# Opening's row sums, split bias loads and earlier row products in a one-core decoder block

## The chip, the core and the metric

The kernel runs on one core of one Trainium2 chip. The time of a run is the device time of one execution in microseconds (us). PE is the matrix engine (its weight loads are listed apart, as PEld), DVE the vector engine, ACT the scalar engine, POOL the GpSimd engine, and SP the queue that issues the transfers (DMA) of the weights.

## The reference

One decoder block for 256 tokens of width 1024, in f32. Cut to what matters:

```python
h = rmsnorm(x, g) * (1 + scale(c)) + shift(c)     # scale, shift, gates: silu(c) @ W_ada, row products
z = h @ W_in                                      # q, k's, v's, NSA gates, MLA latents, merge gates
kc = gelu(blocks(k) @ w1) @ w2                    # compression; vc alike
o  = NSA(q, kc, vc, k_slc, ..) + T5 bias in each logit
m  = MLA(latents)                                 # 8 heads
x1 = x + gate * (merge(o, m) @ W_o)
y  = x1 + gate2 * ffn(norm(x1) modulated)         # gate branch with causal conv of width 3, silu
```

`W_ada` is [1024, 6 * 1024]. A row product multiplies one 128 x 1024 piece of it by silu(c) on DVE and sums along the row: one column of `mod` each.

## The kernel before, in words

Each f32 matrix product is made of three products of a high and a low part (`hi` on ACT, `lo` on DVE). The tokens lie along the free axis, 256 of them; the width is tiled by 128, so that k runs from 0 to 7.

The stages, with their times in the profile: opening (to 16 us): `opening()` squares x on ACT, adds pairs of tiles on DVE (L316), sums the rows with 1-column matmuls on PE (`ssq.reduce`, tile `ms`), `rstd_col` makes the inverse root (ACT, then a power on POOL, L272), `rstd_bc` writes it on a diagonal (ACT, L279) and broadcasts it with one matmul (`ms<-sq,ones`). `busy(n)` issues n matmuls whose result nobody reads (`lg<-ones`); their numbers stand in `WARM`. `modulate(k)` makes the row products of tile k (`gemv`, L375), its scale column `am` (ACT, L402), its shift (L407) and the modulated tile `hf`, and from it the parts `hh[k]`, `hl[k]`.

Then the products with k = 0 to 7 (16 to 62 us), weights `wA` streaming; values and gates (63 to 80 us): eight pieces `wvg` of 280 KB, 12 matmuls for each k, with the query tiles evacuated between them (L441, L442). Up to here the order of each engine is that of the code. `fetch()` issues the next piece on SP; its buffer is one of a ring of five, so an issue waits until DVE has made the low part of the piece that lay there. The T5 bias is read back from `vdr` in DRAM in four transfers of 512 KB (L521) into the tiles `BT`; attention reads them at L905.

From 80 us a scheduler orders the instructions by priorities. Attention of the first token mixer runs in pairs by `ORDER`; between its steps stands other work in the order of `WORK`: C0 to C3 (products of the compression, weights `cw` and `wc`, tile `ms` for C0), L, N, M (latents), and A, one row product (`ada_rest`) of the 32 pieces `adaR`. `ada_load` issues a piece into a ring of two (`ADB`), after `mark`. Then come the MLA heads (L1027 and around), the row products still left, the output projection, the feed-forward part (243 to 452 us) and the tail.

SP issues all transfers in one order. The program also makes an issue wait for the transfer eight issues before it.

Of the kernel before, what the change touches and what calls it, by code (L numbers as in the profile page):

```python
# [9 lines left out]
F32 = mybir.dt.float32  # L10
F32R = mybir.dt.float32r
I32 = mybir.dt.int32
AF = mybir.ActivationFunctionType
# [20 lines left out]
C_MASK, C_VM, C_ROWV, C_IF, C_SGN = 0, 384, 392, 393, 394  # L34
N_CST = 395

WARM = (5, 2, 2, 3, 3)
PD = 4
ENG2 = "vv"
LATE = 1  # L40
# [7 lines left out]
PK = "W D G LG TT EX SC TU PC V PJ EQ ET EK EV TB CM ME TA".split()  # L48
TAE = "pp"
TE = "aaaavvaa"  # L50
WORK = "C0 A A A A A A A L0 C1 L1 A C2 A L2 C3 N M0 KR CK CS M1 A CR M2 Q0 CL UK A A Q1 M3 M7 M5 M6 UV M4"
ORDER = "T00 L00 L01 T01 F L10 V00 F V01 F L11 T11 T10 F V10 F V11 C"


def body(tc, a, out, dbg=None):
    nc = tc.nc
    with ExitStack() as ctx:
# [20 lines left out]
        def s4(dt, shape=(128, 4, 256)):  # L78
            return sp.tile(list(shape), dt, tag="s4", name=nm("s4"))
# [112 lines left out]
        def mm(o, l, r, start, stop, **kw):  # L192
            nc.tensor.matmul(o, l, r, start=start, stop=stop, **kw)  # L193
# [74 lines left out]
        def rstd_col(ssq, width):  # L268

            v = tp.tile([128, 4], F32, tag="rv", name=nm("rv"))  # L270
            nc.scalar.activation(v[:, 0:2], ssq.ps[:, 0:2], AF.Identity, scale=1.0 / width, bias=eps[:])
            nc.gpsimd.tensor_tensor(v[:, 2:4], v[:, 0:2], mhalf[:], ALU.pow)  # L272
            return v[:, 2:4]
# [12 lines left out]
        def busy(n):  # L286

            for i in range(n):
                mm(warm[:, 0:128], ones[:], ones[:], True, True)

        cond = cp.tile([128, 8], F32, name="cond")
        crow = cp.tile([128, 1024], F32, name="crow")
        ssq = Squares(4)
        xsq = big(F32)
        psv = bank("o")
        vdr = dp.tile([16, 384], F32, name="vdr")
# [2 lines left out]
        def opening():  # L299

            nc.scalar.activation(cth[:], par[:, C_C:C_C + 8], AF.Tanh, scale=0.5)
            nc.vector.scalar_tensor_tensor(cond[:], cth[:], 1.0, par[:, C_C:C_C + 8], ALU.add, ALU.mult)
            nc.vector.tensor_scalar(cond[:], cond[:], 0.5, None, ALU.mult)

            busy(WARM[0])
            for c in range(2):
                ps = bank("pt")
                for i in range(4):
                    mm(ps[:, i * 128:i * 128 + 128], free(cond[:, 4 * c + i:4 * c + i + 1], [[0, 128]]), ident, True, True)
                nc.vector.tensor_copy(crow[:, c * 512:c * 512 + 512], ps[:])  # L310
            for h in range(2):
                busy(WARM[1 + h])
                for j in range(2):
                    t = xsq.t[h][:, 2 * j:2 * j + 2, :]
                    nc.scalar.activation(t, xT.t[h][:, 2 * j:2 * j + 2, :], AF.Square)
                    nc.vector.tensor_tensor(t[:, 0, :], t[:, 0, :], t[:, 1, :], ALU.add)  # L316
                    ssq.reduce(t[:, 0, :], h == 0 and j == 0, h == 1 and j == 1)
            mm(psv[0:16, 0:384], tabx[:], oneh[:], True, True)

        rst = t1("rst", bufs=1)  # L320

# [72 lines left out]

        def modulate(k, r=None):

            for j in (1, 0):
                gemv(mod[:, 8 * j + k:8 * j + k + 1], ads.pop((k, j))[:])
            am = tp.tile([128, 1], F32, tag="am", name=nm("am"))
            if r is None:  # L400
                v = rstd_col(ssq, D)
            nc.scalar.activation(am[:], mod[:, 8 + k:9 + k], AF.Identity, scale=par[:, C_GMIX + k:C_GMIX + k + 1],  # L402
                                 bias=sb1[:, k:k + 1])
            if r is None:
                r = rstd_bc(ssq, D, v=v)
                busy(WARM[4])
            nc.scalar.activation(mod[:, k:k + 1], mod[:, k:k + 1], AF.Identity, bias=par[:, C_ADAB + k:C_ADAB + k + 1])  # L407
            hfs[k] = t1("hf")
            nc.vector.scalar_tensor_tensor(hfs[k][:], xT[:, k, :], am[:], r, ALU.mult, ALU.mult)
            return r  # L410
# [61 lines left out]

        with tc.manual_schedule(engines={EN.DVE, EN.Activation, EN.PE, EN.SP}):
            opening()
            rsp = modulate(0)
            head()
            one = dict(skip_group_check=True)

            def products(k, c, w):
                wh, wl = w  # L480
                tiles = [(8 * c + m, slice(m * 128, m * 128 + 128)) for m in range(8)]
                if k == 0:

                    for x, y in ((wh, hh), (wh, hl), (wl, hh)):
                        for mt, sl in tiles:
                            mm(accp(mt), x[:, sl], y[:, k, :], x is wh and y is hh and mt % 2 == 0, False, **one)
                else:
                    for mt, sl in tiles:
                        mm3(accp(mt), wh[:, sl], wl[:, sl], hh[:, k, :], hl[:, k, :], False, k == 7, **one)

            for k in range(8):
                part_hi(k)
                if k == 0:
                    nc.scalar.activation(rst[:], rsp, AF.Copy)
                    nc.scalar.activation(vec[:], psv[0:16, 0:384], AF.Copy, scale=-1.0)
                    nc.gpsimd.dma_start(vdr[:], vec[:])
                if k < 5:
                    fetch_ada(k + 3)
                    fetch()
                    fetch()  # L500
                if k == 0:
                    part_lo(k)
                w = rest()
                if k:
                    part_lo(k)
                head()
                products(k, 0, w)
                if k < 6:
                    w = rest()
                    head()  # L510
                    products(k, 1, w)
                if k < 7:
                    modulate(k + 1, rst[:])

            fetch()
            fetch()
            fetch()
            BT = [[s4(F32) for _ in range(2)] for _ in range(2)]
            vd = vdr[:]
            for i in range(4):  # L520
                nc.sync.dma_start(BT[i // 2][i % 2][:], bass.AP(tensor=vd.tensor, offset=vd.offset + i * 4 * 384,  # L521
                                                                  ap=[[1, 128], [384, 4], [1, 256]]))
            w = rest()
            head()
            products(6, 1, w)
            w = rest()
            products(7, 1, w)
            for gp in range(2):
                for br in (1, 0):
                    k_evac(br, gp)  # L530
            for i in range(2):
                head()
                pending.append(rest())
            t_evac(0)
            t_evac(1)


            VST = s4(F32, (128, 2, 2, 4, 64))
            gate = cp.tile([128, 2, 48], F32, name="gate")
            vps = [bank(t) for t in ("lg", "lg", "pt", "pt")]  # L540
            queries = [(i, j) for i in (1, 3, 2, 0) for j in range(2)]
            for k in range(8):
                wh, wl = pending.pop(0)
                if k < 5:
                    mark = fetch()

                for tt in (1, 0):
                    for c in range(2):
                        sl = slice(c * 280, (c + 1) * 280)
                        o = vps[tt * 2 + c][:, 0:280]  # L550
                        ts_ = slice(tt * 128, tt * 128 + 128)
                        mm(o, hh[:, k, ts_], wh[:, sl], k == 0, False)
                        mm(o, hl[:, k, ts_], wh[:, sl], False, False)
                        mm(o, hh[:, k, ts_], wl[:, sl], False, k == 7)
                if k < 6:
                    head()
                    pending.append(rest())
                i, j = queries.pop(0)
                q_evac(i, (j,))
            for tt in (1, 0):  # L560
                for c in range(2):
                    ps = vps[tt * 2 + c]
                    nc.scalar.activation(VST[:, tt, c, :, :], ps[:, 0:256].rearrange("p (g d) -> p g d", g=4), AF.Copy)
                    ga = nc.scalar.activation(gate[:, tt, c * 24:(c + 1) * 24], ps[:, 256:280], AF.Tanh, scale=0.5).ins
            gv = nc.vector.tensor_scalar(gate[:], gate[:], 0.5, 0.5, ALU.mult, ALU.add).ins
# [417 lines left out]
        for h in range(8):  # L983
# [42 lines left out]
            nc.vector.tensor_tensor(ON[:, h, :], ON[:, h, :], tb[:], ALU.add)  # L1026
            nc.scalar.activation(YH[:, h, :], ON[:, h, :], AF.Copy)  # L1027
            nc.vector.tensor_tensor(YL[:, h, :], ON[:, h, :], YH[:, h, :], ALU.subtract)

        for q in range(3):  # L1030
            while 8 * q + 8 > 32 - len(rest) - len(loaded):
                ada_rest()

        nc.vector.tensor_scalar(mod[:, 16:24], mod[:, 16:24], 0.5, None, ALU.mult)
        af = cp.tile([128, 8], F32, name="af")
# [228 lines left out]
```

## Time and profile before

| what | value |
|---|---|
| median of 3 runs | 466.67 us (466.03 to 468.31) |
| profiled execution | 466.78 us, span 465.0 us |
| mean granted clock of PE | 0.976 |
| busy: PE, PEld | 445.4 us (96%), 418.4 us (90%) |
| busy: DVE, ACT, POOL | 362.9 us (78%), 289.1 us (62%), 27.0 us (6%) |

The span is the time from the first to the last instruction; about 1.8 us of the profiled execution lie around it. A granted clock of 1.00 is 2.4 GHz, 0.5 is 1.2 GHz. "[3.28 <-ACT hi L150]" behind a row means that the engine stood for 3.28 us ahead of it, and that what ended the wait was ACT's `hi` of line 150.

### The profile page before, as it was taken

The numbers are of one execution on the slowest core, as the hardware profiler recorded it, in microseconds if no ns is written. First come the engines' busy times: TensorE is split into PE (matmuls) and PEld (weight loads), VectorE is DVE, ScalarE is ACT, GpSimd is POOL, SyncE is SP. The second block draws the span as 40 slices with busy tenths as digits, with TensorE's granted clock in tenths as the row PEclk, the third lists the DMA queues.
The fourth block names the chain that finished last, engine by engine and source line by source line (L and its number), as shares of the span: only waits on it lengthen the run. The fifth ranks groups of instructions, "written<-read, shape, count | busy, mean of one in ns | idle before, by whom it ended". The sixth has DMA issues, their size and how long they took to land.

```text
span 465.0 us, 9372 instructions
## 1 busy us (share of the span) xinstructions
PE 445.4 (96%) x3516; PEld 418.4 (90%) x3516; DVE 362.9 (78%) x852; ACT 289.1 (62%) x629; POOL 27.0 (6%) x47
## 2 busy tenths in 40 slices
PE   7899989999989999999979999999999999999994
PEld 6899988777869769899969999999999999999994
DVE  4799867888777888899988878877877877867643
ACT  4655457898799986656646766655655645645322
POOL 2100060030000201000000000000000000000002
PEclk9799998999999999999988999999999999999997
DMA  8999598778742358987865836564564564663002
GB/s 286 412 409 397 176 284 268 290 269 291 265 155 92 111 173 275 331 300 246 285 229 175 270 116 203 177 210 165 181 204 160 185 204 156 189 216 96 2 0 92
DMA packets 31134, 99.34 MB, mean 214 GB/s; under 512 B 4245, under 2 KB 6757, under 8 KB 31088
## 3 DMA queue, kind: packets, MB, share of 16 engines
q1 hardware_dynamic: 30064, 96.76, 61.8%
q0 software_dynamic: 1024, 1.98, 1.8%
q8 instruction: 28, 0.46, 0.4%
q14 instruction: 18, 0.15, 0.1%
HBM read 96.01 MB, written 1.14 MB: 209 GB/s over the span
## 4 chain that ended last, share of the span: by engine, by line
PE 73%; DMA 13%; DVE 6%; ACT 4%; issue 3%; POOL 1%; SPq 0%; POOLq 0%; DVEq 0%; ACTq 0%
PE mm L193 30%; PE lg L193 11%; PE ms L193 11%; PE o L193 11%; PE pt L193 8%; DMA s<-in_wA 4%; DMA raw<-in_wvg 3%; PE pt L930 2%; DMA raw<-in_wA 2%; DMA raw<-in_wo 1%; DVE lo L154 1%; DMA ad<-in_adaR 1%; ACT hi L150 1%; DVE L L375 1%; DMA raw<-in_wg 1%
## 5 line engine op out<-in xcount | busy, mean ns | idle before, releaser
L193 PE MATMUL mm<-s,hi 128*128 128x256 f32 x552 | 107.7, 293 | 4.1 <-ACT s L1027 1.9
L135 DVE TENSOR_TENSOR s<-raw,s 128x1024 fp32r<-128x1024 f32 x66 | 80.5, 1221 | 21.1 <-PE mm L193 17.6
L193 PEld LDWEIGHTS mm<-s,hi 128*128 128x128 f32 x552 | 87.0, 193 | 8.6 <-ACT s L1027 2.1
L193 PE MATMUL mm<-s,s 128*128 128x258 f32 (+1 forms) x544 | 94.2, 283 | 0.0
L134 ACT ACTIVATE s<-raw 128x1024 fp32r<-128x1024 f32 x66 | 69.3, 1051 | 28.3 <-PE mm L193 23.7
L193 PEld LDWEIGHTS mm<-s,s 128*128 128x128 f32 x544 | 77.6, 189 | 0.1
L193 PE MATMUL mm<-s,lo 128*128 128x256 f32 x268 | 77.5, 291 | 0.0
L193 PEld LDWEIGHTS mm<-s,lo 128*128 128x128 f32 x268 | 51.6, 194 | 1.3 <-issue 0.8
L193 PE MATMUL o<-s,s 128*128 128x258 f32 (+1 forms) x272 | 48.2, 283 | 0.0
L193 PE MATMUL ms<-s,s 128*128 128x258 f32 x264 | 46.0, 283 | 0.0
L375 DVE CUSTOM_DVE_ANT_0 ad<-ad,crow 128x1024 f32<-128x1024 f32 x36 | 43.5, 1217 | 2.9 <-DMA ad<-in_adaR 2.9
L134 ACT ACTIVATE hi<-raw 128x1024 fp32r<-128x1024 f32 (+1 forms) x31 | 32.3, 1045 | 19.9 <-issue 16.0
L193 PEld LDWEIGHTS o<-s,s 128*128 128x128 f32 x272 | 39.1, 189 | 0.0
L135 DVE TENSOR_TENSOR lo<-raw,hi 128x1024 fp32r<-128x1024 f32 (+1 forms) x31 | 37.3, 1202 | 1.9 <-ACT hi L134 1.9
L193 PEld LDWEIGHTS ms<-s,s 128*128 128x128 f32 x264 | 37.8, 189 | 0.0
L193 PE MATMUL pt<-zh,s 128*128 128x256 f32 x176 | 34.8, 281 | 0.0
L193 PE MATMUL lg<-zh,s 128*128 128x256 f32 x176 | 34.8, 281 | 0.0
L909 ACT ACTIVATE L<-L,sm 128x128 f32<-128x128 f32 (+1 forms) x64 | 28.4, 449 | 1.0 <-DVE sm L905 0.9
L905 DVE CUSTOM_DVE_ANT_0 L<-lg,s 128x128 f32<-128x128 f32 (+1 forms) x64 | 20.8, 350 | 10.0 <-PE lg L193 8.5
L193 PEld LDWEIGHTS pt<-zh,s 128*128 128x128 f32 x176 | 28.6, 189 | 0.0
L193 PEld LDWEIGHTS lg<-zh,s 128*128 128x128 f32 x176 | 28.5, 188 | 0.0
L193 PE MATMUL lg<-s,s 128*128 128x256 f32 (+4 forms) x104 | 28.1, 352 | 0.0
(253 smaller groups left out, 856.2 us busy)
## 6 DMA issues: line engine op xcount, KB each, us to landing
ad<-in_adaR SPq DMA_DIRECT2D x32, 512.0 KB, 4.7
raw<-in_wg SPq DMA_DIRECT2D x22, 512.0 KB, 3.5
raw<-in_wu SPq DMA_DIRECT2D x22, 512.0 KB, 4.3
raw<-in_wd SPq DMA_DIRECT2D x22, 512.0 KB, 4.5
raw<-in_wm SPq DMA_DIRECT2D x16, 512.0 KB, 4.7
L<-in_adaA SPq DMA_DIRECT2D x12, 512.0 KB, 9.0
raw<-in_wA SPq DMA_DIRECT2D x10, 512.0 KB, 9.2
raw<-in_cw SPq DMA_DIRECT2D x8, 512.0 KB, 5.5
```

The costliest lines, as they stand in the source:

```text
L134: nc.scalar.activation(hi[:], raw[:], AF.Copy)
L135: nc.vector.tensor_tensor(lo[:], raw[:], hi[:], ALU.subtract)
L150: nc.scalar.activation(raws[0][1][:], raw[:], AF.Copy)
L154: nc.vector.tensor_tensor(lo[:], raw[:], hi[:], ALU.subtract)
L193: nc.tensor.matmul(o, l, r, start=start, stop=stop, **kw)
L375: nc.vector.tensor_tensor_reduce(out=ad, in0=ad, in1=crow[:], scale=1.0, scalar=0.0, op0=ALU.mult, op1=ALU.add, accum_out=dst)
L905: nc.vector.tensor_tensor_reduce(out=L[:, br, j, 0:nk], in0=lgj[:, br, :], in1=bias_view(2 * t + j, qt), scale=1.0, scalar=3e38, op0=ALU.a ...
L909: nc.scalar.activation(L[:, br, j, 0:nk], L[:, br, j, 0:nk], AF.Exp, scale=-1.0, bias=sm[:, i:i + 1], accum_out=sm[:, 4 + i:5 + i])
L930: nc.tensor.transpose(pt[:, (kb * 2 + j) * 128:(kb * 2 + j) * 128 + 128], self.L[qt][:, br, j, kb * 128:kb * 128 + 128], ident)
```

## The change

Four edits. (a) The opening: the adds on DVE go, PE sums the rows of all eight squared tiles, and the filler matmuls stand elsewhere. (b) In `modulate(0)`, the inverse root and the diagonals stand ahead of the row products and of `am`; the shift of k = 0 is an add on DVE. (c) The four bias loads stand around the pieces of `wvg`: one behind the second piece, one behind the third, two behind the last piece (`mark` is now the last bias load). (d) `WORK` has five more A, and the heads' loop has one row product for each head instead of all of them behind the loop.

```diff
-WARM = (5, 2, 2, 3, 3)
+WARM = (5, 2, 0, 4, 7)
-WORK = "C0 A A A A A A A L0 C1 L1 A C2 A L2 C3 N M0 KR CK CS M1 A CR M2 Q0 CL UK A A Q1 M3 M7 M5 M6 UV M4"
+WORK = "C0 A A A A A A A L0 C1 L1 A C2 A L2 C3 N M0 KR CK CS M1 A CR M2 Q0 CL UK A A Q1 M3 A M7 A M5 A M6 A UV A M4"
...
-        ssq = Squares(4)
+        ssq = Squares(8)
...
                     nc.scalar.activation(t, xT.t[h][:, 2 * j:2 * j + 2, :], AF.Square)
-                    nc.vector.tensor_tensor(t[:, 0, :], t[:, 0, :], t[:, 1, :], ALU.add)
-                    ssq.reduce(t[:, 0, :], h == 0 and j == 0, h == 1 and j == 1)
+                    for i in range(2):
+                        ssq.reduce(t[:, i, :], h == i == j == 0, h == i == j == 1)
             mm(psv[0:16, 0:384], tabx[:], oneh[:], True, True)
+            busy(WARM[3])
...
+            if r is None:
+                v = rstd_col(ssq, D)
             for j in (1, 0):
                 gemv(mod[:, 8 * j + k:8 * j + k + 1], ads.pop((k, j))[:])
...
+            opened = r is not None
+            if not opened:
+                r = rstd_bc(ssq, D, v=v)
+                busy(WARM[4])
...
+            if opened:
+                nc.scalar.activation(sh[0], sh[0], AF.Identity, bias=sh[1])
+            else:
+                nc.vector.tensor_tensor(sh[0], sh[0], sh[1], ALU.add)
...
             fetch()
             fetch()
+            fetch_bias(0)
             fetch()
-            for i in range(4):
-                nc.sync.dma_start(BT[i // 2][i % 2][:], ...
+            fetch_bias(1)
...
                 if k < 5:
-                    mark = fetch()
+                    fetch()
+                if k == 4:
+                    fetch_bias(2)
+                    mark = fetch_bias(3)
...
-        for q in range(3):
-            while 8 * q + 8 > 32 - len(rest) - len(loaded):
+            if h < 7 and len(rest) + len(loaded) > 8:
                 ada_rest()
+
+        while len(rest) + len(loaded) > 8:
+            ada_rest()
```

On SP, the transfers of the values stage before (`in_wvg` the values' pieces, `vdr` the bias, `in_pos` the positions, `in_cw` the first weights of C0):

```order
39 L521 DMA s_119_725<-vdr 128x4x256
40 L521 DMA s_120_726<-vdr 128x4x256
41 L521 DMA s_121_727<-vdr 128x4x256
42 L521 DMA s_122_728<-vdr 128x4x256
43 L145 DMA raw_822<-in_wvg 128x560
47 L145 DMA raw_902<-in_wvg 128x560
50 L330 DMA mg_982<-in_pos 32x64 x4
51 L332 DMA cst<-in_cst 128x395
52 L115 DMA raw_1109<-in_cw 128x1024
53 L115 DMA raw_1111<-in_cw 128x1024
```

and of the change:

```order
37 L145 DMA raw_735<-in_wvg 128x560
38 L525 DMA s_116_729<-vdr 128x4x256
39 L145 DMA raw_738<-in_wvg 128x560
40 L525 DMA s_117_730<-vdr 128x4x256
41 L145 DMA raw_830<-in_wvg 128x560
45 L145 DMA raw_910<-in_wvg 128x560
46 L115 DMA raw_1119<-in_cw 128x1024
47 L525 DMA s_118_731<-vdr 128x4x256
48 L525 DMA s_119_732<-vdr 128x4x256
51 L331 DMA mg_992<-in_pos 32x64 x4
52 L333 DMA cst<-in_cst 128x395
53 L115 DMA raw_1121<-in_cw 128x1024
```

One bias load now stands ahead of the third piece, one behind it, and two behind the last piece and the first weights of C0; the second weights of C0 (raw_1121, raw_1111 before) stand behind these two.

On PE, the start of attention before (`ms` is C0, `lg` logits, `mm` a later product):

```order
472 L193 MATMUL ms_1108<-raw_1111,s_44_154 64x256
473 L193 MATMUL ms_1108<-raw_1109,s_43_153 64x256
474 L193 MATMUL lg_1036<-s_39_149,s_35_145 128x256
476 L193 MATMUL ms_1108<-raw_1111,s_44_154 64x256
477 L193 MATMUL ms_1108<-raw_1109,s_43_153 64x256
478 L193 MATMUL lg_1064<-s_39_149,s_35_145 128x512
480 L193 MATMUL lg_1084<-s_39_149,s_35_145 128x256
482 L193 MATMUL ms_1108<-raw_1111,s_44_154 64x256
483 L193 MATMUL ms_1108<-raw_1109,s_43_153 64x256
484 L193 MATMUL ms_1108<-raw_1111,s_44_154 64x256
```

and of the change:

```order
472 L193 MATMUL lg_1046<-s_39_149,s_35_145 128x256
474 L193 MATMUL lg_1074<-s_39_149,s_35_145 128x512
476 L193 MATMUL lg_1094<-s_39_149,s_35_145 128x256
478 L193 MATMUL ms_1118<-raw_1121,s_44_154 64x256
479 L193 MATMUL ms_1118<-raw_1119,s_43_153 64x256
480 L193 MATMUL ms_1118<-raw_1121,s_44_154 64x256
482 L193 MATMUL ms_1118<-raw_1121,s_44_154 64x256
484 L193 MATMUL ms_1118<-raw_1121,s_44_154 64x256
485 L193 MATMUL lg_1137<-s_39_149,s_35_145 128x512
```

All logits of the first pair now stand ahead of the first product with the second weights of C0.

On SP behind that, before (`in_cw`, `in_wc` weights of the compression, `in_wm` of the latents, `in_adaR` pieces of the row products):

```order
61 L115 DMA raw_1290<-in_cw 128x1024
62 L115 DMA raw_1350<-in_wc 128x1024
63 L601 DMA ad_1149<-in_adaR 128x1024
64 L601 DMA ad_1152<-in_adaR 128x1024
65 L115 DMA raw_1356<-in_cw 128x1024
66 L115 DMA raw_1410<-in_cw 128x1024
```

and of the change:

```order
61 L614 DMA ad_1159<-in_adaR 128x1024
62 L614 DMA ad_1162<-in_adaR 128x1024
63 L115 DMA raw_1300<-in_cw 128x1024
64 L614 DMA ad_1165<-in_adaR 128x1024
65 L115 DMA raw_1360<-in_wc 128x1024
66 L115 DMA raw_1366<-in_cw 128x1024
```

Three pieces for row products stand ahead of weights of the compression that they stood behind. From the 103rd transfer on SP, and from about 200 us of the profile on all engines, the order of before and of the change is the same.

## Rows read from the trace of the kernel before

**Rows 1.** The page: busy us, share of the span, instructions.

```profile
PE 445.4 (96%) x3516; PEld 418.4 (90%) x3516; DVE 362.9 (78%) x852; ACT 289.1 (62%) x629; POOL 27.0 (6%) x47
```

**Rows 2.** Windows by stage: length, busy by engine, granted clock, DMA share, GB/s.

```profile
13.00:20.00 7.00, 6.63 (x28) 6.27 (x29) 4.74 (x7) 4.75 (x10) 0.56 (x1) 0.51 1.03 413
20.00:54.00 34.00, 34.00 (x291) 34.00 (x291) 33.71 (x51) 18.97 (x33) 0.00 (x0) 1.00 0.91 351
50.00:54.50 4.50, 4.50 (x40) 4.46 (x38) 4.49 (x8) 2.42 (x6) 0.00 (x0) 1.00 0.24 64
70.90:74.50 3.60, 3.50 (x15) 3.50 (x16) 3.44 (x6) 3.00 (x5) 0.00 (x0) 0.53 0.81 152
80.20:127.00 46.80, 46.80 (x346) 36.28 (x345) 37.30 (x154) 37.99 (x121) 4.74 (x10) 1.00 0.76 282
```

**Rows 3.** Timeline of the opening: start, us, engine, line, what [idle before].

```profile
7.64 1.53 DVE L316 TENSOR_TENSOR s<-s 128x256 f32<-128x256 f32 x4
8.12 1.05 PE L193 MATMUL ms<-ones,s 128*128 128x1 f32 x8 [0.67 <-DVE s L316]
10.88 1.70 POOL L272 TENSOR_TENSOR rv<-rv,mhalf 128x2 f32<-128x2 f32 x1 [7.19 <-ACT rv L271]
12.62 0.69 ACT L279 ACTIVATE sq<-par,rv 128x128 f32<-128x128 f32 x2 [1.26 <-POOL rv L272]
13.37 1.22 PE L193 MATMUL ms<-sq,ones 128*128 128x256 f32 x2 [2.11 <-ACT sq L279]
14.38 1.49 PE L193 MATMUL lg<-ones 128*128 128x128 f32 x6
14.63 0.48 DVE L409 SCALAR_TENSOR_TENSOR hf<-s,am,ms 128x256 f32<-128x256 f32 x1 [2.60 <-PE ms L193]
```

**Rows 4.** Chain of waits, values stage: start, us, what.

```profile
55.69 1.03 DVE lo L154
56.72 12.68 DMA raw<-in_wvg
71.00 1.29 PE pt L193 x4
75.64 0.78 PE pt L193 x6
80.28 0.64 PE ms L193 x2
```

**Rows 5.** Timeline of SP: issues of the values stage.

```profile
54.54 2.08 SPq L521 DMA_DIRECT2D s<-vdr  x4
56.72 9.84 SPq L145 DMA_DIRECT2D raw<-in_wvg  x5
74.51 1.34 SPq L115 DMA_DIRECT2D raw<-in_cw  x2
```

**Rows 6.** Issues: KB, us to landing (third piece; first bias; second `cw`).

```profile
raw<-in_wvg SPq DMA_DIRECT2D x1, 280.0 KB, 2.9
s<-vdr SPq DMA_DIRECT2D x1, 512.0 KB, 4.5
raw<-in_cw SPq DMA_DIRECT2D x1, 512.0 KB, 4.5
```

**Rows 7.** Timeline of DVE, values stage.

```profile
64.67 1.54 DVE L154 TENSOR_TENSOR lo<-raw,hi 128x560 fp32r<-128x560 f32 x1 [1.54 <-ACT hi L150]
66.24 0.69 DVE L442 SCALAR_TENSOR_TENSOR s<-mm,s 64x512 fp32r<-64x512 f32 x1
70.20 0.74 DVE L154 TENSOR_TENSOR lo<-raw,hi 128x560 fp32r<-128x560 f32 x1 [3.28 <-ACT hi L150]
```

**Rows 8.** Timeline of PE, start of attention.

```profile
81.75 0.71 PE L193 MATMUL ms<-raw,s 128*64 128x256 f32 x4
84.36 1.14 PE L193 MATMUL ms<-raw,s 128*64 128x256 f32 x6
```

**Rows 9.** The page: issues, KB, median us to landing.

```profile
ad<-in_adaR SPq DMA_DIRECT2D x32, 512.0 KB, 4.7
```

More of the change, by code (lines that the diff above doesn't have):

```diff
@@ L399, in modulate @@
             am = tp.tile([128, 1], F32, tag="am", name=nm("am"))
-            if r is None:
-                v = rstd_col(ssq, D)
+            opened = r is not None
+            if not opened:
+                r = rstd_bc(ssq, D, v=v)
+                busy(WARM[4])
             nc.scalar.activation(am[:], mod[:, 8 + k:9 + k], AF.Identity, scale=par[:, C_GMIX + k:C_GMIX + k + 1],
                                  bias=sb1[:, k:k + 1])
[L404 to L407, printed above, removed]
+            sh = mod[:, k:k + 1], par[:, C_ADAB + k:C_ADAB + k + 1]
+            if opened:
+                nc.scalar.activation(sh[0], sh[0], AF.Identity, bias=sh[1])
+            else:
+                nc.vector.tensor_tensor(sh[0], sh[0], sh[1], ALU.add)
             hfs[k] = t1("hf")
@@ L513, in body, with fetch_bias @@
                     modulate(k + 1, rst[:])
+            BT = [[s4(F32) for _ in range(2)] for _ in range(2)]
+            vd = vdr[:]
+            def fetch_bias(i):
+                return nc.sync.dma_start(BT[i // 2][i % 2][:], bass.AP(tensor=vd.tensor, offset=vd.offset + i * 4 * 384,
+                                                                       ap=[[1, 128], [384, 4], [1, 256]])).ins
             fetch()
             fetch()
+            fetch_bias(0)
             fetch()
-            BT = [[s4(F32) for _ in range(2)] for _ in range(2)]
-            vd = vdr[:]
-            for i in range(4):
-                nc.sync.dma_start(BT[i // 2][i % 2][:], bass.AP(tensor=vd.tensor, offset=vd.offset + i * 4 * 384,
-                                                                  ap=[[1, 128], [384, 4], [1, 256]]))
+            fetch_bias(1)
             w = rest()
```

## The prediction

> **What bounds the kernel now.** I read the page first: PE is busy 96% of the span and its weight loads 90%, DVE 78% [rows 1]. So a stage is worth what it takes from PE's stream, and the question is where PE stands or runs at half clock. Windows by stage give that [rows 2]: in 13 to 20 us the granted clock is 0.51; from 20 to 54 PE and DVE are both full (34.00 and 33.71 of 34.00 us); in 50 to 54.5 the DMA moves only 64 GB/s; in 70.9 to 74.5 the clock is 0.53 again; from 80.2 to 127 PE is busy 46.80 of 46.80 us. The change touches the first three places and the order of the last.
>
> The timeline of the opening [rows 3] shows a chain: adds on DVE, row sums, power on POOL (1.70 us), diagonals, broadcast, `hf` at 14.63. PE stands 2.11 us before the broadcast and then runs it at half clock. The chain of waits in the values stage [rows 4] shows the largest single wait that the change aims at: the fourth values' piece is issued at 56.72, when DVE has given its buffer back, and takes 12.68 us to land. Ahead of it on SP lie the four bias loads, issued from 54.54 on [rows 5]: 2 MB. A piece of the same size, alone, lands 2.9 us after its issue [rows 6]. DVE waits 3.28 us for the high part of that piece, PE is released at 71.00, and its clock has fallen meanwhile [rows 7, 2].
>
> **The opening.** Four adds (1.53 us on DVE, beside the squares) go [rows 3]. PE makes eight more row sums; each is two instructions in the trace, and eight take 1.05 us, 0.13 each [rows 3]. All 32 take 3.8 to 4.2 us (0.12, as the starts of the rows lie, to 0.13). The adds no longer stand between squares and sums: PE stood 0.67 us for them ahead of 8.12, so the sums begin at about 7.2 and end at 11.0 to 11.4. The power then starts about 0.5 us later than before, at 11.4, and ends at 13.1. The diagonals, which began at 12.62 and took 0.69, end at 13.8 instead of 13.3. The broadcast took 1.22 us at clock 0.51, which makes 0.6 at full clock. So `hf` comes at about 14.4 in place of 14.63: 0.2 us sooner. The condition is the clock. PE's gap before the broadcast shrinks from 2.11 us to about 1 us, since four fillers stand behind the sums. I take that the clock stays up. Bound on the other side: it falls anyway; then the broadcast takes 1.2 us, and the 14 filler instructions behind it (six took 1.49 us, 0.25 each) take 3.5 us instead of 1.8, so that PE starts k = 0 about 2 us late, of which the DVE-paced products behind take up over half: +0.8. From 15.7 to 57 DVE has hardly a gap (33.71 of 34 us), so at the end of the products only DVE's shift counts. Term **-0.1** (-0.6 to +0.8). The shift of k = 0 on DVE is one column, and the ACT instruction that goes stood behind `am`, off the chain: nothing.
>
> By the Trainium skill (Perfetto Trace Analysis, Identifying the Most-Contended Engine), the engine with the highest occupancy is to be relieved first, and PE's headroom is judged by its weight loads. By that rule this edit is wrong, since it puts work on the engine with 90% and takes it from one with 78%; the sum would be 2.1 us worse, by the row's 0.13 us for 16 instructions [rows 3]. The trace shows that PE stands just there [rows 3], so the sum takes nothing for it; it is a rival below.
>
> **The bias split.** Bias 0 is issued at about 50, where the DMA is nearly idle [rows 2], and lands before 54.5. Bias 1 follows the third piece at 54.5 and lands 4.5 us later, as the first one did [rows 6]. The fourth piece is still issued at 56.7, because DVE's buffer release sets that [rows 4], but has only bias 1 beside it: between 2.9 us and 5 us, landing at 60 to 61.7. ACT and DVE then make its parts in their written order. ACT needs 0.67 us for it behind its work on the third piece, done by 66. DVE is free after 66.24 + 0.69 = 66.93 [rows 7]; the low part takes 0.74 us, or 1.54 if it runs as the one at 64.67 did, which lay beside POOL's adds [rows 7]. It ends at 67.7 to 68.5. PE ends k = 2 at 67.8, so it waits 0 to 0.7 us instead of 3.2, and the clock stays up. The five k left take 0.78 + 0.77 us twice over: each k is two such pairs of 0.77, 1.55 us [rows 4]. From 68.5 that is 76.25. Before, the last ended at 80.2 [rows 4]. So values end **4.0 us sooner** (3.3 to 4.6).
>
> **What it gives back.** Two bias loads now stand ahead of the small loads and of C0's second weights on SP. Bias 2 and 3 go out once the first weights of C0 have a buffer, that is when the low part of the fourth piece is made: 68.5, then 69. Three transfers of 512 KB lie together there, and I take 6 us for the last (one took 4.5 [rows 6]; the fourth piece of the values, queued behind four, took 12.7 [rows 4]): 75. The last of the position loads and `cst` wait for the transfer eight issues before, which are just these two; so `cst` goes out at 75.3 and the second weights at 76.0, against 75.5 to 75.8 before, the last of two issues that started at 74.51 and took 1.34 us [rows 5]. They land 4.5 us later [rows 6], at 80.3 (79 to 82).
>
> In the new order on PE all logits of the first pair stand ahead of the first product with these weights. Logits and one product take 0.3 + 2.2 us from 76.4, to about 79.1; PE then stands 1.2 us, to 80.3. Behind it stand seven products, each two instructions, 0.16 us apiece (six in 1.14 with the tail [rows 8]): 2.25 us, to 82.55. Before, the same work ended at 84.36 + 1.07 = 85.4 [rows 8]. So of 4.0 us, **2.9 stay** at this point (bounds 1.7 and 4.2 by the landing).
>
> **Row products.** Five A more in the list and one for each head move pieces, not their number: 32 before and after. The order shows that the loads of three pieces pass weights of the compression on SP, and the uses of these weights move back on PE; from about 200 us on every engine has its old order. A row product needs its piece 4.7 us after the issue [rows 9]; if it is wanted sooner, DVE stands, and behind it the softmax sums. PE is full from 80 to 127 with DVE at 37.30 and ACT at 37.99 of 46.8 us [rows 2]: 9 us of slack on each to cover one such wait. I take **0** (0 to +3.5 for each wait that nothing covers).
>
> **Sum.** -0.1 - 4.0 + 1.1 + 0 = -3.0. From the profiled 466.78 that is **463.8**; the profiled execution lies 0.1 above the median of 466.67, which leaves the number as it is. A difference under 0.5%, 2.3 us, can't be told from no change here; the bound for faster is 464.3.
>
> **The rivals.**
> - A, the sum above: 463.8. Its own range, by the landing of C0's second weights and the opening, is 462.2 to 465.2.
> - B, PE doesn't stand for these weights (they land by 79), and the opening gives 0.5: -0.5 - 4.2 = -4.7, with a packing no worse, 462.0. For it: positions and `cst` are small. Against: their issue hangs on the two bias loads.
> - C, weights pace the start of attention. All weights behind C0's second are issued 0.3 to 0.7 us later than before, though PE reaches them 3 us sooner. If they set the pace up to 91 us, the 2.9 us shrink to under 1: 466.2. For it: DMA share 0.76 in the window of 80.2 to 127 [rows 2], and landings of 4.5 us. Against: PE has no gap there now, so weights arrived in time with room that the trace doesn't show.
> - D, slower: the row products' loads. Three now pass weights on SP, and a row product stands on DVE with less than 4.7 us since its load's issue. Each that directly follows the row product before it (1.2 us) costs up to 3.5 us of DVE, ahead of softmax sums that PE waits for. One such wait eats the gain (467.3); it decides from the second on: 466.8 - 3.0 + 7.0 = 470.8, with a part covered 469.5. Against: DVE's slack of 9 us.
> - E, PE pays for the opening's sums: 16 more instructions at 0.13 us end on the path, 2.1 us, because the products behind them are PE's and not DVE's to pace (both are full there [rows 2]): 466.8 - 3.0 + 2.1 = 465.9. This is what the skill's rule named above would make of the edit.
>
> **How the numbers follow.** A 0.45, B 0.16, C 0.23, D 0.11, E 0.05. The predicted time is A's. Faster by over 0.5% are B and somewhat over seven tenths of A (its range passes the bound by 0.9 us): 0.49. Slower is D with little else: 0.12. The rest, 0.39, lies within. The range leaves out D and the low end of B: 461.0 to 467.6, the upper end being C with one uncovered wait.
>
> **What would show it.** Right: no wait of ACT for the fourth values' piece, a landing near 60 to 62, a granted clock of 1.00 from 67 to 76, the last values' matmul near 76.3; PE standing about a microsecond ahead of the first C0 product with second weights, near 80; C0 done near 82.6. In the opening, power from about 11.3, full clock from 13 to 20, `hf` near 14.4. Wrong would be: the second weights landing after 82, DVE waits on `ad` of over 2 us between 85 and 127, a clock of 0.5 in the opening, or an end of PE's work at 127 us shifted by less than 2 us.

## The result and the profile after

The changed kernel takes 470.21 us (median of 16 runs, 467.13 to 478.11), the kernel before 466.63 us on the same chips (16 runs, 464.78 to 469.55): a ratio of 1.0057, 95% interval 1.0033 to 1.0080. It is slower by 2.7 us by the ratio (3.6 between the medians); a gain of 3.0 us was forecast, and 470.2 lies outside the range. Three disturbed runs of the changed kernel of over 476 us, the profiled one among them, are left out of the ratio, and the rows below are of a second profiled execution (469.48 us, span 467.7; the first experiment below).

Windows by stage of the changed kernel (columns as in [rows 2]; 75 to 87 and 238 to 250 us are new):

```profile
13.00:20.00 7.00, 6.86 (x48) 6.36 (x48) 4.36 (x7) 4.95 (x9) 0.56 (x1) 0.84 1.02 410
50.00:54.50 4.50, 4.50 (x39) 4.36 (x38) 4.50 (x9) 2.72 (x6) 0.00 (x0) 1.00 0.61 188
70.90:74.50 3.60, 3.60 (x30) 3.60 (x29) 3.44 (x6) 2.94 (x5) 0.00 (x0) 1.00 1.03 286
75.00:80.00 5.00, 3.23 (x18) 2.18 (x16) 2.51 (x8) 2.33 (x10) 0.00 (x0) 1.00 0.78 135
80.00:87.00 7.00, 5.93 (x20) 3.49 (x20) 3.96 (x31) 6.28 (x21) 0.00 (x0) 0.51 0.98 349
80.20:127.00 46.80, 45.15 (x313) 34.09 (x314) 35.32 (x148) 38.58 (x119) 4.81 (x10) 0.93 0.80 288
238.00:250.00 12.00, 8.43 (x48) 7.64 (x48) 8.84 (x18) 5.49 (x9) 0.00 (x0) 0.75 0.54 169
```

The same windows of the kernel before, where they are new:

```profile
75.00:80.00 5.00, 5.00 (x41) 5.00 (x40) 3.92 (x6) 3.27 (x10) 0.00 (x0) 1.00 0.92 307
80.00:87.00 7.00, 7.00 (x37) 4.34 (x36) 5.53 (x32) 5.55 (x22) 0.00 (x0) 1.00 0.91 358
238.00:250.00 12.00, 8.70 (x46) 8.05 (x45) 8.56 (x15) 7.45 (x12) 0.00 (x0) 0.72 0.54 172
```

The stretch of half clock at 70.9 to 74.5 [rows 2] is gone, as forecast. A new one stands at 80 to 87: PE was busy 3.23 of 5 us ahead of it and then ran at 0.51. An old one, which the prediction left aside, stands near 240 in both kernels.

Timeline of the opening after, which answers to [rows 3]:

```profile
9.03 1.95 PE L193 MATMUL ms<-ones,s 128*128 128x1 f32 x16 [0.43 <-ACT s L315]
11.35 1.61 POOL L272 TENSOR_TENSOR rv<-rv,mhalf 128x2 f32<-128x2 f32 x1 [7.59 <-ACT rv L271]
11.65 1.95 PE L193 MATMUL lg<-ones 128*128 128x128 f32 x8
13.73 1.22 PE L193 MATMUL ms<-sq,ones 128*128 128x256 f32 x2
14.75 1.96 PE L193 MATMUL lg<-ones 128*128 128x128 f32 x14
15.06 0.48 DVE L415 SCALAR_TENSOR_TENSOR hf<-s,am,ms 128x256 f32<-128x256 f32 x1 [2.48 <-PE ms L193]
16.47 0.81 PE L193 MATMUL lg<-s,hi 128*128 128x256 f32 x4
```

The power starts at 11.35, as forecast (11.4). But the first eight fillers take 1.95 us, 0.24 each, and the broadcast 1.22 us: PE is at half clock there. `hf` comes at 15.06 instead of 14.4, and the first product at 16.47 behind the 14 other fillers, against 15.76 before. Its four instructions then take 0.81 us for 1.22 before, so PE catches up; on DVE, each row from 16 to 65 us starts 0.4 us later than the same row before.

Timeline of SP after, values stage (answers to [rows 5]), then of PE and DVE at the start of attention (answers to [rows 8]):

```profile
56.18 10.79 SPq L145 DMA_DIRECT2D raw<-in_wvg  x5
68.46 0.33 SPq L115 DMA_DIRECT2D raw<-in_cw  x1
68.84 0.98 SPq L525 DMA_DIRECT2D s<-vdr  x2
72.08 2.47 SPq L331 DMA_DIRECT2D mg<-in_pos  x4
78.18 0.35 SPq L333 DMA_DIRECT2D cst<-in_cst  x1
79.07 0.35 SPq L115 DMA_DIRECT2D raw<-in_cw  x1
...
76.42 0.71 PE L193 MATMUL ms<-raw,s 128*64 128x256 f32 x2
78.05 1.10 PE L193 MATMUL lg<-s,s 128*128 128x256 f32 x4 [0.92 <-ACT gate L577]
80.28 2.40 PE L193 MATMUL lg<-s,s 128*128 128x256 f32 x6 [1.14 <-DVE sm L918]
83.47 3.62 PE L193 MATMUL ms<-raw,s 128*64 128x256 f32 x14 [0.79 <-DMA raw<-in_cw]
79.49 0.20 DVE L336 CAST mg<-mg 128x64 f32<-128x64 int32 x1 [0.90 <-DMA mg<-in_pos]
```

Values end at 76.4 (forecast 76.3). Then `cst`, which waits for the last bias load, goes out at 78.18, C0's second weights at 79.07, and PE reaches them at 83.47. Ahead of that DVE stood for the positions, with the softmax sums of the first pair behind its cast, and PE's logits stood 1.14 us for these sums. C0's 14 instructions ran at 0.26 us each and ended at 83.47 + 3.62 = 87.1, against 85.5 before [rows 8].

Between 190 and 207 us PE falls back by another 1.6 us against before. DVE waits there for the pieces of row products (nowhere more than 1.02 us in the kernel before):

```profile
198.98 1.23 DVE L376 CUSTOM_DVE_ANT_0 ad<-ad,crow 128x1024 f32<-128x1024 f32 x1 [2.02 <-DMA ad<-in_adaR]
```

### The profile page after: what moved, and what is told of

Its sections match the earlier page's. It is cut to its first block, busy times and chain, and to the rows that moved or that the text cites. A ratio compares the mean times of both kernels' runs of the same rounds, so it can differ in the third digit from the quotient of the medians.

```text
span 474.5 us, 9422 instructions
## 1 busy us (share of the span) xinstructions
PE 453.4 (96%) x3544; PEld 425.3 (90%) x3544; DVE 362.6 (76%) x849; ACT 289.8 (61%) x628; POOL 26.9 (6%) x47
## 3 DMA queue, kind: packets, MB, share of 16 engines
HBM read 96.01 MB, written 1.14 MB: 205 GB/s over the span
## 4 chain that ended last, share of the span: by engine, by line
PE 49%; DMA 2%; DVE 2%; issue 2%; ACT 1%; POOL 0%; POOLq 0%; DVEq 0%; ACTq 0%
PE mm L193 21%; PE o L193 7%; PE lg L193 7%; PE ms L193 7%; PE pt L193 7%; DMA raw<-in_wg 1%; DMA ad<-in_adaR 1%; DVE ad L376 1%; DVE lo L135 0%; POOL s L1155 0%; PE pt L1021 0%; ACT s L134 0%; ACT hi L134 0%; DVE s L1041 0%; DVE L L1168 0%
## 5 line engine op out<-in xcount | busy, mean ns | idle before, releaser
L193 PEld LDWEIGHTS mm<-s,hi 128*128 128x128 f32 x552 | 88.0, 195 | 8.3 <-ACT s L1040 3.0
L193 PEld LDWEIGHTS mm<-s,s 128*128 128x128 f32 x544 | 77.7, 189 | 0.1
```

## The experiments

**The parts alone (four kernels).** The changed kernel again; then the bias split alone; the opening's edits (a) and (b) alone; the change without its last edit (d). Their diffs are the pieces of the diff above.

> The changed kernel once more, for a profile of an undisturbed execution. The profile at hand has the values' last matmul 2.2 us sooner than before although the opening is 2.1 us late, and then PE standing between 78.7 and 85.4 us for position loads (a cast on DVE ahead of the softmax sums) and for C0's second weights. Theory G (the give-back on SP): the same here, second weights landing at 83 to 86 us, wherever the opening ends. Theory O (the opening): hf again 2 us late with a granted clock near 0.6 in 13 to 20 us. Theory S (the scheduler's order): the losses lie behind 100 us, in PE waits of the attention stage that before did not have. Time 468 to 471.

> The bias split alone; opening, list and heads' loop as before. Theory G: values end 3.5 to 4.5 us sooner than before's 80.2, the second weights of C0 land at 81 to 84 instead of 80.0, PE stands 3 to 5 us between 77 and 84, and the time is 465 to 468. Theory O: all the loss was the opening's, so this kernel gains, 463 to 465. Theory S: the new order behind 85 us loses of itself, 468 to 470, with PE waits behind 100 us.

> The opening's edits alone (row sums on PE, fillers moved, power and diagonals ahead of the row products); everything behind has its old order. Theory O: PE's clock falls all the same, hf 1.5 to 2.5 us late, time 1.5 to 2.5 us over before: 468 to 469. Theory G and S: the opening ends as before within 0.5 us, time 466.2 to 467.

> The change without its last edit (list and heads' loop of before), with opening and bias split. All theories: the last edit moves only a few row products on DVE and little else, so this is within 0.7 us of the changed kernel (469 to 471). If row products made the loss, it is 466 to 468.

Measured, against 466.94 us of before: the change again 470.87 (1.0072, 1.0046 to 1.0099); bias split 463.63 (0.9938, 0.9912 to 0.9963); opening 468.88 (1.0048, 1.0026 to 1.0071); without (d) 465.34 (0.9951, 0.9929 to 0.9973). In the first, C0's second weights landed at 83.3, as theory G said; `hf` was 0.4 us late and not 2, as theory O had it. The third took the time that theory O gave it, but with `hf` only 0.7 us late (15.35) instead of 1.5 to 2.5. The second looked like a gain of the split, and the fourth came as no theory said: without (d) the loss was gone. But the windows of the bias split alone have the loss at 80 to 87, too, and the gain elsewhere:

```profile
80.00:87.00 7.00, 5.97 (x21) 3.57 (x22) 3.47 (x27) 5.91 (x21) 0.00 (x0) 0.52 0.98 380
238.00:250.00 12.00, 11.16 (x91) 10.59 (x90) 10.32 (x18) 8.88 (x15) 0.00 (x0) 1.00 0.56 178
```

At 238 to 250 us it has no half clock and twice the instructions on PE. The timeline of ACT there in the changed kernel shows what stands ahead of the last head's `YH` (L1040):

```profile
242.50 1.06 ACT L134 ACTIVATE s<-raw 128x1024 fp32r<-128x1024 f32 x1 [5.33 <-DMA raw<-in_wg]
243.47 0.40 ACT L1040 ACTIVATE s<-s 128x256 fp32r<-128x256 f32 x1
```

ACT waits 5.33 us for the first weights of the feed-forward part, and `YH`, for which PE waits, is queued behind. The kernel before has the same pair (a wait of 4.50 us). In the order of the bias split alone, and of the change without (d), the two rows have changed places; with (d) they stand as before. ACT's rows of the bias split alone:

```order
290 L1034 ACTIVATE s_439_2489<-s_160_1019 128x256
291 L134 ACTIVATE s_579_3215<-raw_3213 128x1024
```

and of the changed kernel:

```order
289 L134 ACTIVATE s_579_3225<-raw_3223 128x1024
290 L1040 ACTIVATE s_444_2515<-s_160_1029 128x256
```

**The exchange of these two rows.** It was made by itself in the kernel before and in the changed kernel:

```diff
+        hold = []
...
+            yl_ = nc.scalar.activation(YH[:, h, :], ON[:, h, :], AF.Copy).ins
+            if h == 7:
+                hold.append(yl_)
...
-                with prio("W"):
+                with prio("W"), tc.issue_after(hold[0]) if late and hold else nullcontext():
                     nc.scalar.activation(hi[:], raw[:], AF.Copy)
```

> The kernel before with one thing more: ACT's work on the first weights of the feed-forward part is held back behind the last head's YH. Rows on PE, DVE and ACT change only near 240 us, none on SP. Theory L (late order): of the bias split's time, 5 us come from just this exchange of two rows on ACT, so this kernel gains 4 to 5.5 us, 461 to 462.5, and the stretch of half clock near 238 to 248 is gone. Rival (the bias split's own gain at the values was kept): no change, 466 to 467.

> The changed kernel with the same exchange near 240 us and nothing else. Theory L: 4 to 5.5 us under the changed kernel, 465 to 466.5, about what it is without its last edit. Rival (the last edit's row products cost the 5 us themselves): 469.5 to 471 as the changed kernel.

Measured: before with the exchange 460.56 us (0.9871, 0.9840 to 0.9901), the changed kernel with it 463.86 (0.9941, 0.9915 to 0.9968). Theory L holds, and is larger than the 4 to 5.5 us expected: 6.0 us by the ratio (6.4 between the medians), and in the changed kernel 5.4 to 6.1 by the ratios. Timeline of ACT, and below it the window, of before with the exchange:

```profile
237.15 0.42 ACT L1027 ACTIVATE s<-s 128x256 fp32r<-128x256 f32 x1 [3.76 <-DVE s L1026]
238.01 1.06 ACT L134 ACTIVATE s<-raw 128x1024 fp32r<-128x1024 f32 x1 [0.44 <-DMA raw<-in_wg]
```

```profile
238.00:250.00 12.00, 11.65 (x98) 11.38 (x97) 11.40 (x20) 10.51 (x18) 0.00 (x0) 1.00 0.59 186
```

`YH` no longer waits for that load, the clock stays at 1.00, and PE begins 98 instructions in these 12 us instead of 46.

So the bias split alone must be held against 460.56: it costs 3.1 us (463.63), where the first comparison seemed to show a gain of 3.3. By the starts of the same instructions in these two profiles, PE is 2.4 us behind at 90 us, where C0 has ended, 2.0 at 187 and 2.6 at the end. And (d) by itself costs nothing that the times can tell: 463.86 with it (0.9941) and 465.34 without (0.9951), both with the good order.

In the profile of the changed kernel with the exchange the clock stayed at 1.00 behind 80 us, though PE waited there:

```profile
84.61 1.97 PE L193 MATMUL ms<-raw,s 128*64 128x256 f32 x14 [1.93 <-DMA raw<-in_cw]
```

C0's 14 instructions took 1.97 us, where the other four profiles with bias 2 and 3 ahead of the small loads have 3.6 to 3.7. So the fallen clock adds 1.7 us in some executions; the wait for the second weights is there in all of them.

**Bias 2 and 3 late.** They are issued behind the positions, `cst` and C0's second weights (with the exchange):

```diff
-                    fetch()
-                if k == 4:
-                    fetch_bias(2)
-                    mark = fetch_bias(3)
+                    mark = fetch()
...
-            tables()
+            ci = tables()
+        with prio("TB"), tc.issue_after(ci):
+            fetch_bias(2)
+            fetch_bias(3)
```

> The bias split, but bias 2 and 3 issued behind the position loads, cst and C0's second weights, as these are read by later pairs only; with the exchange near 240 us. Theory G (positions, cst and C0's second weights queued behind two bias loads give the values' gain back): the values end 4 us before 80.2, the second weights land at 79 or sooner, PE keeps at least 2.5 of the 4 us, and the time is 2.5 to 4 us under that of before with the exchange: 458 to 460. Rival (the attention stage is bound by later weights, so nothing of the 4 us can be kept): 461 to 463.

Measured: 460.62 us (0.9859, 0.9832 to 0.9885), equal to before with the exchange. Theory G is right on the place (second weights landed at 77.7, C0 done at 82.1), but its 458 to 460 was missed: the 3.1 us are back, but no more. The window shows full clock and a full PE where the change had half clock:

```profile
75.00:80.00 5.00, 4.09 (x23) 2.44 (x21) 3.18 (x17) 3.01 (x10) 0.00 (x0) 1.00 0.96 330
80.00:87.00 7.00, 7.00 (x53) 5.87 (x52) 6.33 (x37) 7.00 (x30) 0.00 (x0) 1.00 1.04 407
```

**Row sums and fillers.** First the sums with the change's fillers, then with the fillers of before:

```diff
-WARM = (5, 2, 0, 4, 7)
+WARM = (5, 2, 2, 0, 3)
```

> Of the opening's edits only the row sums on PE and the moved fillers; the order of power, diagonals and row products, and all behind, as before. The opening's edits together cost 1.9 us over before, though the profile shows their lead of 1 to 2 us at 75 us lost by 85. Theory P (PE's sums and fillers are the cost): 467.5 to 469. Theory R (the row products behind the power are): 466.3 to 467.

> The kernel before with the row sums all on PE but its own fillers (none behind the sums, three behind the broadcast). With the change's fillers the products began 0.7 to 2.7 us later than before. Theory F (fillers at half clock stand ahead of the products): products begin as before within 0.4 us, and the time is 466 to 467.3. Rival P (the sums themselves cost): 468 to 469, as with the fillers.

Measured: with the change's fillers 468.48 us against 466.99 (1.0046, 1.0016 to 1.0077), without them 466.86 against 467.63 (0.9992, 0.9963 to 1.0020). Both times came as theories P and F said: the sums cost nothing that the times can tell, with the fillers they do (the two intervals overlap by a hair, from 1.0016 to 1.0020). The opening's edits together came out at 1.0048, so edit (b) adds nothing. Timeline of PE with the fillers, and below it without:

```profile
13.22 2.07 PE L193 MATMUL lg<-ones 128*128 128x128 f32 x8
15.09 1.06 PE L193 MATMUL ms<-sq,ones 128*128 128x256 f32 x2
15.94 2.75 PE L193 MATMUL lg<-ones 128*128 128x128 f32 x14
18.44 0.80 PE L193 MATMUL lg<-s,hi 128*128 128x256 f32 x4
```

```profile
14.49 1.22 PE L193 MATMUL ms<-sq,ones 128*128 128x256 f32 x2 [2.00 <-ACT sq L279]
15.51 1.49 PE L193 MATMUL lg<-ones 128*128 128x128 f32 x6
16.89 1.22 PE L193 MATMUL lg<-s,hi 128*128 128x256 f32 x4
```

The first product comes at 18.44 with the fillers and at 16.89 without. The expected 0.4 us of before's 15.76 was missed. The later second half of x (squared from 9.11 instead of 7.56) doesn't explain it: in the kernel with bias 2 and 3 late, whose opening is that of before, it was squared from 8.95, and the first product came at

```profile
15.47 1.22 PE L193 MATMUL lg<-s,hi 128*128 128x256 f32 x4
```

In the nine profiles with the opening of before the first product comes at 15.1 to 15.9; with the sums on PE and the change's fillers at 16.5 to 19.0; with the sums and the fillers of before at 16.9 and, in the mended change below, 17.1. So the profiles show a delay by the sums as well; these last two, though, are of executions of 469.9 and 465.9 us, where the medians are 466.9 and 461.5. That the fillers cost and the sums don't rests on the times alone.

**Where the lead at 85 us goes (five kernels).** The kernel with bias 2 and 3 late ends C0 at 82.1 us, 3.4 us sooner than before [rows 8] and 2.6 sooner than before with the exchange (84.8), and is no faster at the end than that one. Three ideas were tried: the loads of the row products in the heads (left out in both kernels), the spread of the row products (edit (d) added), and their work on DVE (left out as well; the last piece of the diff stands in these two kernels only).

```diff
-                ad = st.tile([128, 1024], F32, tag="ad", name=nm("ad"), bufs=ADB)
-                with tc.issue_after(mark):
-                    nc.sync.dma_start(ad[:], a["adaR"][q, t])
-                loaded.append((16 + 8 * q, t, ad))
+                if 8 * q + t < 18:
+                    ad = st.tile([128, 1024], F32, tag="ad", name=nm("ad"), bufs=ADB)
+                    ...
+                    lastad[:] = [ad]
+                loaded.append((16 + 8 * q, t, lastad[0]))
...
+        nc.gpsimd.memset(mod[:, 34:48], 0.0)
...
+            if o + t < 34:
                 with tc.issue_after(gv):
                     gemv(mod[:, o + t:o + t + 1], ad[:])
```

> The kernel before with the exchange near 240 us, and with the last 14 of the 32 row products reading a piece that is already there: 14 loads of 512 KB are left out (their results are not the reference's), the DVE work stays. Theory W (loads of row products set the pace of the heads, 178 to 238 us): the waits on these loads in that stretch (some 3 us on DVE) go, and the time falls by 1 to 2.5 us under the same kernel with its loads, to 458 to 459.5. Rival (they are covered): 460 to 461.

> The bias split with bias 2 and 3 late and the exchange near 240 us, and the same 14 loads left out. The kernel with these loads leads by 3 us at 197 us and has lost the lead by 213. Theory W: the DVE wait of 2.6 us at 199 us is gone, the lead lasts to the end, and the time is 2.5 to 4 us under that of the kernel before with the exchange and fewer loads: 454.5 to 456.5. Rival (the new order of the heads loses the lead): within 1 us of it.

> The bias split with bias 2 and 3 late, the exchange near 240 us, and the change's last edit (list and one row product for each head). Theory W: row products spread so that they ask for their loads no faster than these land would keep some of the lead, 458 to 460; if they are asked for as closely as before, 460 to 461. Rival (the last edit itself costs, as it seemed in the change): over 464.

> The kernel before with the exchange near 240 us and without the last 14 row products: loads and DVE work are left out, so the output isn't the reference's. Theory V (DVE is full in the heads): 14 times 1.22 us of DVE go from a stretch that DVE sets, and the time falls well under the 459.2 of the kernel with fewer loads only, to 455 to 457.5. Rival (PE or the order sets the heads): 458.5 to 459.5.

> The bias split with bias 2 and 3 late, the exchange near 240 us, and without the last 14 row products. Theory V: the lead of 3 us at 197 us now lasts, so 2 to 3.5 us under the kernel before with the same left out. Rival (the order of the attention stage and the heads loses it): within 1 us of it.

Measured: fewer loads, 459.21 us (0.9832, 0.9788 to 0.9877) and with the late bias 458.83 (0.9819, 0.9779 to 0.9859); (d) added, 461.10 (0.9838, 0.9785 to 0.9892); fewer products, 460.07 (0.9850, 0.9825 to 0.9875) and with the late bias 460.50 (0.9859, 0.9819 to 0.9898). Without the loads the kernel before came out as theory W said (458 to 459.5), but the other one didn't (454.5 to 456.5), and the two that leave out the same loads and the DVE work are no faster than these. What the loads and the DVE work are worth can't be told from nothing here. The spread of (d) kept nothing of the lead. Theories W and V fall as its explanation: in no pair does the lead last. Windows of the kernel before with fewer products, then of the one with late bias and fewer products:

```profile
75.00:127.00 52.00, 52.00 (x386) 41.35 (x385) 41.21 (x162) 41.62 (x130) 4.75 (x10) 1.00 0.81 285
127.00:178.00 51.00, 48.76 (x398) 38.76 (x396) 41.23 (x156) 45.76 (x143) 4.75 (x9) 1.00 0.44 142
190.00:210.00 20.00, 19.92 (x146) 18.47 (x145) 13.16 (x31) 13.36 (x32) 0.00 (x0) 1.00 0.51 159
```

```profile
75.00:127.00 52.00, 50.56 (x362) 38.53 (x361) 38.80 (x157) 42.40 (x138) 5.54 (x11) 1.00 0.87 298
127.00:178.00 51.00, 48.12 (x404) 39.80 (x403) 42.12 (x157) 45.41 (x135) 5.74 (x11) 1.00 0.43 138
190.00:210.00 20.00, 18.57 (x140) 17.30 (x139) 13.92 (x35) 11.95 (x28) 0.00 (x0) 1.00 0.52 159
```

PE stands 0 + 2.24 + 0.08 = 2.3 us in the first and 1.44 + 2.88 + 1.43 = 5.75 us in the second: 3.4 us more. The lead was 4.3 us where the values end (75.84 against 80.12). It goes in single waits, mostly for ACT (0.92 us for the gate ahead of the first logits, 1.35 us ahead of a product near 193 us, five of 0.3 to 0.7 between 127 and 178, where ACT is busy 45 of 51 us in both). Whether ACT's load there or the places that the scheduler chose make them was not told apart: that stays open.

**The change mended.** All three at once in the changed kernel: fillers of before, bias 2 and 3 late, the exchange.

> The changed kernel with three things mended: the fillers of before (none behind the sums, three behind the broadcast), bias 2 and 3 behind the small loads and C0's second weights, and the exchange near 240 us. If these three are all of the loss, it is with the other kernels that have the exchange: 460 to 461.5. If something of the change still costs: over 462.5.

Measured: 461.49 us (0.9892, 0.9845 to 0.9939), at the upper end of what was expected, with an interval of over 2 us on either side, and 7.7 us under the changed kernel by the ratios. Some 6 us of this are the stall near 240 us, which the kernel before has, too. The rest is the split's and the opening's, and the runs can't tell whether 1 us of their loss remains. No kernel here that computes the reference is clearly faster than before with the exchange alone: 460.56 us.

## Why the prediction was wrong

The step that failed is what the bias split gives back. It was to take 1.1 us of the 4.0 won, and took more than all of them: 3.1 us lost against before with the same order near 240 us, and just these 3.1 come back with bias 2 and 3 behind the small loads. The opening's term failed beside it, and so did the step that what is ahead at 85 us stays. The prediction's sums hold but for the end of its range: C with one uncovered wait of 3.5 us makes 469.7 and not 467.6, and the measured 470.2 lies beyond that, too.

- **The opening**, forecast at -0.1 with +0.8 as its worst, costs 0.48% by itself, 2.2 us (1.2 to 3.3). The step that failed is "I take that the clock stays up". It fell, and the fillers, meant for it, ran at half clock ahead of the products, so that `hf` came 0.4 and 0.7 us late in the two profiles and not 0.2 sooner. That delay lies within the bound; what makes 2.2 us of it isn't shown. In the profile of the opening alone PE is 0.3 us behind before from 82 to 190 us, and the other 1.7 come from 195 to 245, where DVE waits for row products' pieces (1.44 and 1.20 us for 0.63 and 0.55) and ACT for the first feed-forward weights (5.57 us for 4.50). The rule of the Trainium skill weighed there (Perfetto Trace Analysis, Identifying the Most-Contended Engine), to optimize the most contended engine first, spoke against the edit. The time agrees with it only for sums and fillers together (1.0046); for the sums alone it shows no loss (0.9992).
- **The values** came as forecast: 76.4 for 76.3, full clock, the fourth piece no longer waited for.
- **What it gives back** was mis-sized, and by this the sign of the sum: "I take 6 us for the last" was 9 (issued by 69.8, `cst` released at 78.2), so C0's second weights were reached at 83.5 instead of 80.3. Two mechanisms were missing: the cast of the positions, which stands on DVE ahead of the softmax sums, so that the late small load holds up the logits; and the clock, which in most of the profiles fell after PE's waits and made C0's 14 instructions 3.6 us long. C0 ended 1.6 us later than before, not 2.9 sooner.
- **"2.9 stay"** would have failed even with the loads in good order: the kernel with bias 2 and 3 late had the lead and lost it again before the heads' end. PE busy 46.80 of 46.80 us [rows 2] was read to mean that PE sets the pace there, but a sooner PE found ACT, and here and there DVE, less ready. Why they were not is open.
- **Row products** at 0: right by the times, (d) is within their error (some 1.6 us). The rival that ended slower had its mechanism here. DVE does wait 2.02 us for a piece, but near 199 us and not between 85 and 127, where the prediction looked, and it waits 2.60 us there in the kernel with bias 2 and 3 late, which hasn't (d); the pair without the loads didn't keep the lead either.
- **Nothing behind 200 us**: right for the order, and nearly so for the time (the stall near 240 is 0.8 us longer, 5.33 us for 4.50). With (d) the order there is that of before, with a stall that costs about 6 us in both. The prediction saw that the order was the same and didn't ask what it cost.

The parts one on top of the other, by the ratios and with the good order near 240 us in all: before 0.9871, with the split 0.9938, with the opening 0.9951, with (d) 0.9941. Only the first step, 0.67%, is clear of its error of 0.40% (worked out from the two intervals); the opening's 0.13% and (d)'s -0.10% are within theirs (0.34%). So the opening's 2.2 us are shown only for the kernel with the stall near 240.

## What to carry to other kernels

A load that is split and moved to fill an idle stretch must be followed to whatever now stands behind it on the queue, small loads above all, and from there to the in-order engine whose first instruction waits for them. An edit's time alone can be the scheduler's: where a part gains, look for the stretch in which it does, and make that exchange by itself before it is put down to the edit. Time won in one stage need not be kept: here 3.4 of 4.3 us went in waits for engines that were no sooner ready.

## What the runs showed of the hardware

In the change PE waited 1.8 us of 75 to 80 and then ran at a granted clock of 0.51 from 80 to 87; with bias 2 and 3 late it waited 0.9 us of 75 to 80 and kept 1.00. Waits alone don't foretell it: the changed kernel with the exchange waited 0.9 us of 75 to 80 and 2.7 us of 80 to 87, and kept 1.00. The four position loads of 8 KB took 6.1 us to land (median) behind two bias loads, and 2.1 us ahead of them. In the opening the granted clock was under 1.00 in 13 to 20 us in each profile, with fillers or without (0.50 to 0.85). The same power of 256 values on POOL took from 0.71 to 1.70 us in different executions, and the second half of x was squared from 7.56 to 9.61 us on, with no edit that touches its load: differences under 2 us in the opening need more than one profile.
